# Second layer: ten pairs of projection blocks as seven half-products each, in another order

## The chip, the cores and the metric

The kernel runs on one core of one Trainium2 chip. The metric is the device time of one execution in microseconds (us). The median of three runs of the kernel before is 1501.39 us (1498.27 to 1502.47).

## The reference

Two layers are applied to 1024 latent tokens and 256 context tokens, each a row of 1024 values. A layer normalises and modulates the tokens, makes one input projection (1024 columns in, 3616 columns out: the pieces named below), feeds four groups of heads with it, and projects their gated outputs back. Cut to what matters here (calls shortened):

```python
def hybrid_layer(x, ctx, c, c_ctx, norm_g, w_mod, b_mod, w_in, ...):
    mod_x = jax.nn.silu(c) @ w_mod + b_mod
    ...
    hx = modulate(rms_norm(x, norm_g), sh_x, sc_x)
    hc = modulate(rms_norm(ctx, norm_g), sh_c, sc_c)
    (a_q, a_k, a_v, a_g, b_cq, b_ckv, b_kr, b_g,
     c_u, c_v, c_g, d_b, d_c, d_h, d_g) = jnp.split(hx @ w_in, IN_SPLIT_POINTS, axis=-1)
    (a_qc, a_kc, a_vc, ...) = jnp.split(hc @ w_in, IN_SPLIT_POINTS, axis=-1)
    out_a = neighbourhood_attention(heads(a_q), heads(a_k), heads(a_v), ctx keys and values, na_rpb)
    out_b = latent attention on b_cq, b_ckv and the rotated key b_kr
    out_c = spatial_gating(gelu(c_u), gelu(c_v), ...)   # u * (W_s LN(v) + b), in chunks of 128 tokens
    out_d = short_conv(d_b, d_c, d_h, sc_w)             # B * conv3(C * h)
    y = merge_branches([out_a, out_b, out_c, out_d], [a_g, b_g, c_g, d_g], w_out)   # gates through SiLU
    x = x + g_x * y
```

After the second layer only the latent tokens are wanted. Of the context tokens that layer needs the keys and values alone: the pieces ak, av, ckv and kr. The names in the kernel are those of the pieces without the underscore (a_k is ak); a piece of 256 columns is two blocks of 128, ak0 and ak1.

## The kernel before

**Tiling.** Everything is fp32. A product of two fp32 matrices is made of three: each operand is split into a high part (a cast to fp32r) and a low part (what the cast lost), and `mm3` (L172) issues high by high, high by low and low by high for each of 8 slices of the 1024 inputs. The normalised tokens lie in H, in tiles `g` that hold high and low of one slice (128 features) of one chunk. There are three chunks: 0 and 1 with 512 latent tokens each, 2 with the 256 context tokens. A weight block (128x1024) is loaded into `wr` by SP, `split` casts it on ScalarE (ACT) into `wh` (L338) and GpSimd (POOL) subtracts that into `wl` (L343). `proj` then takes 24 matmuls for each chunk into one bank of PSUM (`psb`, issued at L159) and hands the bank to a function that evacuates it. So a block on chunks 0 and 1 is 48 matmuls of 512 columns, and a pair of blocks is 96.

**Order in a layer.** The body of a layer emits cu and cv first: `cu` makes two blocks, `cv_tokens` makes 128 tokens at a time (24 matmuls of 256 columns), applies Gelu on ACT into a `v1` tile, and normalises it on VectorE (DVE): statistics (L479, L481), a reciprocal root whose power is on POOL (L204) and three steps on DVE (L206, L207, L209), then four subtract-and-multiply instructions (L486) into a `g` tile. The pool `v1` has three buffers, and the bias `bs` of the layer holds one. `cv_gate(c)` multiplies the four normalised token tiles of a chunk by a 128x128 matrix (16 small matmuls), adds the bias on DVE (L498) and multiplies into the map on POOL (L501). Then come cg; for j = 0, 1 dc, dh (with the convolution on POOL, L538, and DVE, L540 and L542), db, dg; av in ten tiles of 128 tokens, with copies of the values to scratch in DRAM; ckv with its own statistics (ones matmul on PE, L581 on DVE, power on POOL, transposes on PE); cq; the rotation of the key part of av's tiles on POOL (L650 to L655); ak; the transposes of the rotated keys; aq, bg, ag. `gate` is the evacuation of the gate blocks (Silu on ACT, L449, product on POOL, L451). Results that the attention reads go through tiles `st` (two buffers) to scratch in DRAM.

**What sets the order on an engine.** A scheduler orders each engine's instructions when the kernel is built, by times that it simulates. On the chip each engine takes its list strictly in that order and waits at the first instruction that isn't ready. The attention after the projections is in an order written out by hand, and neither it nor layer 1 is touched by the change.

The evacuation of a block and the split that feeds the next are these lines:

```python
hi, lo = w_block(a["wtb"][l, b_], scale, first_raw.get((l, b_)))
for c in chunks:
    p = PS("b", [CHUNKS[c][1]])
    mm3(p, [(hi[:, kc, :], lo[:, kc, :], hap(c, kc, 0), hap(c, kc, 1)) for kc in range(KC)])
    evac(c, p)
```

## Time and profile before

| | kernel before |
|---|---|
| median of 3 runs | 1501.39 us (1498.27 to 1502.47) |
| profiled execution, its own time | 1498.92 us |
| its span | 1496.8 us |
| mean granted clock of TensorE | 0.990 |
| busy: PE, DVE, ACT, POOL | 1427.9 us (95%), 767.5 (51%), 573.8 (38%), 459.7 (31%) |
| second layer's projections | about 822 to 1150 us of the span |

The span is from the first to the last instruction. A start in a timeline is counted from the span's start. Matmul rows give the time from issue to a modelled end, and these overlap: the rate of a stream of matmuls is the distance from start to start. "<-" behind a row names the work that released it after an idle stretch of its engine.

### The profile page before, as it was taken

The page shows a single profiled execution, that of the slowest core. Times are in us where ns is not written, and L with a number is a line of the kernel's source. Part 1 is how long each engine was busy: PE and PEld are TensorE (multiplying, and loading weights), DVE is VectorE, ACT ScalarE, POOL GpSimd, SP SyncE. Part 2 cuts the span into 40 slices and gives each one's busy share as a digit, 9 for nine tenths or more (in the row PEclk, how much of TensorE's full clock was granted, in tenths as well). Part 3 has the DMA queues.
Part 4 walks back from the last instruction along what each step waited for, and adds up shares of the span by engine and source line. Part 5 has one row for each costly group of instructions (what it writes and reads, how often), then busy time and mean ns, then how long its engine had stood idle before and what let it go on. Part 6 is the DMA issues. An engine that isn't in the chain of part 4 may idle for free.

```text
span 1496.8 us, 23098 instructions
## 1 busy us (share of the span) xinstructions
PE 1427.9 (95%) x8964; PEld 1193.6 (80%) x8964; DVE 767.5 (51%) x1873; ACT 573.8 (38%) x1303; POOL 459.7 (31%) x369
## 2 busy tenths in 40 slices
PE   4999999999998999999999999999999899999987
PEld 2888889988886777677788978898888677778887
DVE  5868656073026677564463752201213677754474
ACT  5512111122226565553442421112223666554542
POOL 2145343141230001536522253412232000155751
PEclk9999999999999999999999999999999999999999
DMA  9513325255361004746433101123474012385241
GB/s 350 199 41 113 120 81 173 99 210 167 127 126 15 1 22 126 152 123 166 140 115 127 36 29 43 54 84 122 155 242 90 1 36 43 99 179 160 71 155 56
DMA packets 80941, 166.45 MB, mean 111 GB/s; under 512 B 8128, under 2 KB 34752, under 8 KB 80704
## 3 DMA queue, kind: packets, MB, share of 16 engines
q1 hardware_dynamic: 63808, 136.66, 27.7%
q0 software_dynamic: 15936, 27.27, 9.1%
q8 instruction: 70, 1.15, 0.3%
q10 hardware_dynamic: 1088, 1.05, 0.2%
q14 instruction: 39, 0.32, 0.1%
HBM read 135.33 MB, written 33.82 MB: 113 GB/s over the span
## 4 chain that ended last, share of the span: by engine, by line
PE 82%; DVE 7%; ACT 3%; issue 3%; POOL 3%; DMA 1%; SPq 0%; DVEq 0%; POOLq 0%; ACTq 0%
PE psb L159 67%; PE pst L162 7%; PE psv L159 7%; PE pst L159 1%; DVE s L827 1%; ACT pt L723 1%; DVE g L486 1%; POOL g L1127 1%; POOL s L204 1%; DVE pt L721 1%; POOL wh L340 1%; DVE s L206 0%; DMA st<-in_nab 0%; DMA wr<-in_wtb 0%; POOL wl L343 0%
## 5 line engine op out<-in xcount | busy, mean ns | idle before, releaser
L159 PE MATMUL psb<-g,wh 128*128 128x512 f32 (+1 forms) x2400 | 685.2, 371 | 1.3 <-ACT g L394 1.3
L159 PEld LDWEIGHTS psb<-g,wh 128*128 128x128 f32 x2400 | 431.2, 189 | 85.7 <-ACT g L394 2.6
L159 PE MATMUL psb<-g,wl 128*128 128x512 f32 (+1 forms) x1200 | 443.5, 370 | 0.0
L159 PEld LDWEIGHTS psb<-g,wl 128*128 128x128 f32 x1200 | 226.1, 188 | 41.3 <-issue 1.0
L343 POOL TENSOR_TENSOR wl<-wr,wh 128x1024 fp32r<-128x1024 f32 (+2 forms) x64 | 149.9, 2344 | 305.2 <-ACT wh L338 297.9
L159 PE MATMUL psb<-g,st 128*128 128x512 f32 (+1 forms) x616 | 159.7, 377 | 17.2 <-DVE g L763 4.5
L827 DVE TENSOR_REDUCE s<-psb 128x1 f32<-128x512 f32 (+1 forms) x200 | 117.2, 591 | 83.7 <-PE psb L159 80.7
L159 PE MATMUL psb<-g,g 128*128 128x256 f32 (+2 forms) x832 | 136.0, 309 | 0.1
L159 PEld LDWEIGHTS psb<-g,st 128*128 128x128 f32 x616 | 96.9, 190 | 43.8 <-issue 14.2
L723 ACT COPY pt<-pst 128x512 f32<-128x512 f32 (+1 forms) x132 | 73.8, 559 | 126.5 <-PE pst L162 126.2
L159 PE MATMUL psv<-pt,g 128*64 128x256 f32 (+1 forms) x1312 | 120.8, 334 | 0.8 <-DVE s L972 0.5
L338 ACT CAST wh<-wr 128x1024 fp32r<-128x1024 f32 (+2 forms) x56 | 56.1, 1006 | 167.4 <-PE psb L159 134.7
L159 PEld LDWEIGHTS psb<-g,g 128*128 128x128 f32 x832 | 113.5, 197 | 6.0 <-issue 3.3
L159 PEld LDWEIGHTS psv<-pt,g 128*64 128x64 f32 x1312 | 79.9, 137 | 32.7 <-issue 9.0
L318 DVE CUSTOM_DVE_ANT_0 tmp<-g,x 128x512 f32<-128x512 f32 x112 | 94.7, 898 | 8.7 <-POOL x L451 7.2
L721 DVE COPY pt<-pst 128x512 f32<-128x512 f32 x132 | 86.2, 653 | 10.0 <-PE pst L162 9.4
L162 PE MATMUL pst<-ident,g 128*128 128x128 f32 x464 | 82.2, 278 | 8.1 <-ACT g L974 3.2
L204 POOL TENSOR_TENSOR s<-s,mhalf 128x4 f32<-128x4 f32 (+3 forms) x35 | 35.7, 1020 | 150.2 <-DVE s L260 59.3
L340 POOL TENSOR_SCALAR wh<-wr 128x1024 fp32r<-128x1024 f32 x16 | 44.3, 2770 | 114.6 <-PE pst L162 66.3
L1157 DVE SCALAR_TENSOR_TENSOR x<-psb,modG,x 128x512 f32<-128x512 f32 (+1 forms) x48 | 29.5, 616 | 91.9 <-PE psb L159 58.2
L162 PEld LDWEIGHTS pst<-ident,g 128*128 128x128 f32 x464 | 55.5, 140 | 25.4 <-ACT g L974 5.3
L159 PE MATMUL psb<-st,g 128*128 128x288 f32 (+1 forms) x456 | 64.3, 289 | 0.0
(183 smaller groups left out, 1837.4 us busy)
## 6 DMA issues: line engine op xcount, KB each, us to landing
g<-in_wmod SPq DMA_DIRECT2D x48, 512.0 KB, 4.5
wr<-in_wtb SPq DMA_DIRECT2D x46, 512.0 KB, 3.8
wr<-in_wout SPq DMA_DIRECT2D x27, 512.0 KB, 3.7
st<-in_nab SPq DMA_DIRECT2D x24, 384.0 KB, 3.5
x<-in_xT SPq DMA_DIRECT2D x32, 256.0 KB, 5.9
g<-scr_q POOLq DMA_DIRECT2D x32, 256.0 KB, 7.0
x<-x SPq DMA_DIRECT2D x24, 256.0 KB, 2.8
g<-scr_k POOLq DMA_DIRECT2D x20, 256.0 KB, 5.4
```

The source lines that it names most:

```text
L159: return self._next(nc.tensor.matmul(*p, **k))
L162: return self._next(nc.tensor.transpose(*p, **k))
L204: pool.tensor_tensor(r0, v, mhalf[:, :n], ALU.pow)
L318: dve.tensor_tensor_reduce(junk, w[:, hf * 512:hf * 512 + 512], crow[cond, hf], 1.0, 0.0, ALU.mult, ALU.add, part[:, i, cond, hf:hf + 1])
L338: act.copy(hi, raw)
L340: pool.tensor_scalar(hi, raw, 1.0, None, ALU.mult)
L343: (pool if lo_eng == "pool" else dve).tensor_tensor(lo, raw, f(hi), ALU.subtract)
L486: dve.tensor_scalar(vns[c][:, i, g, :], gv[:, g, :], mv[:, g, 0:1], r[:, g:g + 1], ALU.subtract, ALU.mult)
L721: dve.tensor_copy(dst, src)
L723: act.copy(dst, src)
L827: dve.reduce_max(st["mx"][:, i:i + 1], s_, AX.X)
L1157: dve.scalar_tensor_tensor(xa, p, mod[l]["G"][:, fb, cond:cond + 1], xa, ALU.mult, ALU.add)
```

## The change

Only layer 2 is changed. Layer 1 keeps the blocks and their order; its code moves into a function `standard`.

**Half-products.** For ten pairs of blocks (cg, dc, dh, db, dg, cq, ak, aq, bg, ag) the two weight blocks and the two latent chunks are read as a 2 by 2 matrix of halves: rows of weights j = 0, 1, halves k = 0, 1 of the 1024 inputs (4 slices each), chunks 0 and 1. Where before the pair was eight half-products of 12 matmuls, `proj2` makes seven of 12, with sums of halves as operands (Strassen's scheme in Winograd's form). Four sums of weight halves are made on DVE for each pair (L693 to L696), and seven half blocks are split by `w_op` (a cast of 128x512 on ACT, a subtraction of 128x512 on POOL) where before two whole blocks were. Between the products ACT and DVE move and add partial results (L701, L703, L708, L713, L718, L721), and an evacuation then often reads SBUF where it read PSUM.

**Token sums.** `right_sums(i)`, for i = 0 to 3, makes the sums of the tokens' halves that all ten pairs use: per i four additions of high and low (L669, three on DVE, one on POOL), four subtractions on DVE (L672) and four splits (cast on ACT, low part on DVE for two and on POOL for two).

**Context.** ak on chunk 2 is made on its own by `block_c`, with its own load of the blocks. **Buffers.** A class `Phase` opens pools for a part of the program: four tiles `o` for some of the sums during the projections, `pt` and `pc` at the beginning and in the attention. The rotated keys and the convolution's input move from `g` to `x` tiles. **Order.** After cu and cv come ckv (chunks 2, 1, 0), ak on the context, av (context tiles, then chunk 1, then chunk 0), the rotation, and the pairs cg, dc, dh, db, dg, cq, ak, aq, bg, ag; `mla_load` and the first attention unit's loads are emitted inside ag.

The diff, cut to its core:

```diff
+    BUFS = {"x": 20, "g": 24, "wr": 2, "wh": 2, "wl": 2, "st": 2, "tmp": 6, "pt": 6, "v1": 3, "pc": 8, "s": 12, "o": 4}
...
+        def w_op(raw):
+            t = T(("wh", "wl")[nop[0] % 2], [2, 512], F32R)
+            nop[0] += 1
+            split(t[:, 0, :], t[:, 1, :], raw)
+            return t.rearrange("p h (k n) -> p h k n", k=4)
+
+        R = {}
+
+        def right_sums(i):
+
+            t = {}
+            for k, (c, kc) in enumerate(((0, i), (1, i), (1, i + 4), (0, i + 4))):
+                t[k] = T("x", [512])
+                (pool if k == 3 else dve).tensor_tensor(t[k], f(H[c, kc][:, 0, :]), f(H[c, kc][:, 1, :]), ALU.add)
+            R["11", i], R["21", i], R["22", i] = H[0, i], H[0, i + 4], H[1, i + 4]
+            for name, o, p_, q_ in (("1", 0, 1, 0), ("3", 1, 2, 1), ("2", 2, 2, 0), ("4", 3, 3, 2)):
+                dve.tensor_tensor(t[o], t[p_], t[q_], ALU.subtract)
+                r = R[name, i] = T("o" if i < 2 and name in "23" else "g", [2, 512], F32R)
+                split(r[:, 0, :], r[:, 1, :], t[o], lo_eng="dve" if name in "12" else "pool")
+
+        def product(p, w, name, first=True):
+            n = 0
+            for i in range(4):
+                r = R[name, i]
+                for wl_, rl_ in ((0, 0), (0, 1), (1, 0)):
+                    pe.matmul(p, w[:, wl_, i, :], r[:, rl_, :], start=first and n == 0, stop=n == 11,
+                              skip_group_check=True)
+                    n += 1
+
+        def proj2(base, evac, mid=None):
+            r = {}
+            for j in range(2):
+                for k in range(2):
+                    r[j, k] = T("x", [512])
+                    sp.dma_start(r[j, k], a["wtb"][l, BLOCKS.index(f"{base}{j}")][:, k * 512:(k + 1) * 512])
+            q = T("wr", [2, 512])
+            a11, a12 = w_op(r[0, 0]), w_op(r[0, 1])
+            dve.tensor_tensor(q[:, 1, :], r[0, 0], r[1, 0], ALU.subtract)
+            dve.tensor_tensor(r[1, 0], r[1, 0], r[1, 1], ALU.add)
+            dve.tensor_tensor(q[:, 0, :], r[1, 0], r[0, 0], ALU.subtract)
+            dve.tensor_tensor(r[0, 1], r[0, 1], q[:, 0, :], ALU.subtract)
+            s2, s1 = w_op(q[:, 0, :]), w_op(r[1, 0])
+            x_, y_ = PS("b", [512]), PS("b", [512])
+            product(x_, a11, "11")
+            m1 = T("tmp", [512])
+            act.copy(m1, x_)
+            product(y_, a12, "21")
+            dve.tensor_tensor(m1, y_, m1, ALU.add)
+            evac(0, m1, 0)
+            s3 = w_op(q[:, 1, :])
+            product(x_, s2, "2", False)
+            u2 = T("tmp", [512])
+            act.copy(u2, x_)
+            s4 = w_op(r[0, 1])
+            z_ = PS("b", [512])
+            product(z_, s1, "1")
+            z5 = T("tmp", [512])
+            dve.tensor_copy(z5, z_)
+            if mid is not None:
+                mid()
+            a22 = w_op(r[1, 1])
+            product(x_, s3, "3", False)
+            dve.tensor_tensor(z5, x_, z5, ALU.add)
+            evac(1, z5, 1)
+            product(z_, s4, "22", False)
+            dve.tensor_tensor(u2, z_, u2, ALU.add)
+            evac(1, u2, 0)
+            product(x_, a22, "4", False)
+            evac(0, x_, 1)
...
+        def paired():
+            right_sums(0)
+            right_sums(1)
+            cv_gate(1)
+            proj("ckv0", (2, 1, 0), ckv_evac)
+            for j in range(2):
+                block_c(f"ak{j}", 2, lambda c, p: k_evac(c, p, j))
+            wav = w_tok(a["wav"][l], 288)
+            for t in (8, 9, 4, 5, 6, 7):
+                av_tile(t, wav)
+            right_sums(2)
+            right_sums(3)
+            for t in range(4):
+                av_tile(t, wav)
+            av_windows()
+            kr = kr_rotate()
+            proj2("cg", lambda c, p, j: gate(c, p, 4 + j))
+            kr_transpose(*kr)
+            proj2("dc", lambda c, p, j: act.copy(map_(6 + j, c), p))
...
+            proj2("dh", conv_in)
...
+            proj2("db", mulb)
+            proj2("dg", lambda c, p, j: gate(c, p, 6 + j))
+            proj2("cq", cq_evac)
+            proj2("ak", k_evac)
+            cq_stats()
+            proj2("aq", lambda c, p, j: q_evac(c, p, j, 0.125))
+            proj2("bg", lambda c, p, j: act.activation(map_(2 + j, c), p, AF.Silu))
...
+            ph = Phase("prj", ("o",))
+            paired()
+        else:
+            standard()
+            ag_weights()
...
-            mla_load()
-        for c in order[:-1]:
-            ag(c)
-            if c == 2:
-                mla_load()
-        units[0].prep()
-        ag(order[-1])
+            proj2("ag", lambda c, p, j: act.activation(map_(j, c), p, AF.Silu), lambda: (mla_load(), units[0].prep()))
+            ph.close()
```

**Where instructions move, on DVE.** In cv's token tiles of chunk 0, before (s are statistics, v is a Gelu tile, g the normalised tokens; s_8499 belongs to the second tile, v_8533 to the third):

```order
L483 TENSOR_SCALAR s_8495<-s_8486 128x4
L206 SCALAR_TENSOR_TENSOR s_8499<-s_8495,s_8497 128x4
L207 TENSOR_TENSOR s_8499<-s_8499,s_8497 128x4
L209 SCALAR_TENSOR_TENSOR s_8502<-s_8499,s_8497 128x4
L479 BN_STATS s_8535<-v_8533 128x6 x3
L486 TENSOR_SCALAR g_8407<-v_8483,s_8486,s_8502 128x64 x4
L479 BN_STATS s_8535<-v_8533 128x6
L481 BN_AGGR s_8536<-s_8535 128x2 x4
L483 TENSOR_SCALAR s_8545<-s_8536 128x4
L206 SCALAR_TENSOR_TENSOR s_8549<-s_8545,s_8547 128x4
```

After (x, o and g are token sums; s_8562 belongs to the third tile v_8546, and v_8596 is the fourth):

```order
L672 TENSOR_TENSOR x_8913<-x_8913,x_8911 128x512
L672 TENSOR_TENSOR x_8937<-x_8937,x_8935 128x512
L357 TENSOR_TENSOR o_8924<-x_8911,o_8924 128x512
L220 SCALAR_TENSOR_TENSOR s_8562<-s_8558,s_8560 128x4
L672 TENSOR_TENSOR x_9410<-x_9410,x_9408 128x512
L357 TENSOR_TENSOR o_8948<-x_8935,o_8948 128x512
L672 TENSOR_TENSOR x_9434<-x_9434,x_9432 128x512
L221 TENSOR_TENSOR s_8562<-s_8562,s_8560 128x4
L223 SCALAR_TENSOR_TENSOR s_8565<-s_8562,s_8560 128x4
L493 BN_STATS s_8598<-v_8596 128x6 x3
L500 TENSOR_SCALAR g_8420<-v_8546,s_8549,s_8565 128x64 x4
L493 BN_STATS s_8598<-v_8596 128x6
```

What moved: these rows are the end of a stretch that begins behind the second tile's first step (L220 after, L206 before); from there to the statistics of v_8596 all 12 additions L669, all 16 subtractions L672 and two low parts (L357) stand between the steps of the second and the third tile.

**On PE, at the gate of cv.** Before, the gate of chunk 0 is followed by cg:

```order
L159 MATMUL psb_8813<-g_8069,g_8272 128x256
L159 MATMUL psb_8863<-tmp_8330,g_8407 64x128 x8
L159 MATMUL psb_8875<-tmp_8330,g_8407 64x128 x8
L159 MATMUL psb_8893<-g_7677,wh_8889 128x512 x2
L159 MATMUL psb_8893<-g_7677,wl_8890 128x512
L159 MATMUL psb_8893<-g_7682,wh_8889 128x512 x2
```

After, the matmuls of chunk 0's gate (g_8420) and the first of chunk 1's (g_8675) stand together, and ckv on the context (psb_8985) follows:

```order
L173 MATMUL psb_8826<-g_8082,g_8285 128x256
L173 MATMUL psb_8876<-tmp_8343,g_8420 64x128 x6
L173 MATMUL psb_8888<-tmp_8343,g_8420 64x128 x6
L173 MATMUL psb_8876<-tmp_8343,g_8420 64x128 x2
L173 MATMUL psb_8888<-tmp_8343,g_8420 64x128 x2
L173 MATMUL psb_8955<-tmp_8343,g_8675 64x128 x2
L173 MATMUL psb_8967<-tmp_8343,g_8675 64x128
L173 MATMUL psb_8985<-g_8307,wh_8981 128x256 x2
L173 MATMUL psb_8985<-g_8307,wl_8982 128x256
```

What moved: three small matmuls on the fifth token tile, the first of chunk 1, now stand ahead of the first block; before, they came after cg0 on both chunks (48 matmuls).

**On PE and POOL, at the rotated keys.** Before, the transposes of the rotated keys (tile g_10142) stand on PE between two blocks, the rotation that makes them much earlier on POOL:

```order
L159 MATMUL psb_10335<-g_8321,wh_10273 128x256 x2
L159 MATMUL psb_10335<-g_8321,wl_10274 128x256
L162 MATMUL pst_10364<-ident_66,g_10142 128x128 x4
L162 MATMUL pst_10373<-ident_66,g_10142 128x128 x4
L159 MATMUL psb_10395<-g_7677,wh_10391 128x512 x2
L159 MATMUL psb_10395<-g_7677,wl_10392 128x512
```

```order
L604 TENSOR_TENSOR x_10035<-x_10035,tmp_10103 128x512
L650 TENSOR_TENSOR tmp_10144<-tmp_9545,tmp_9546 128x256
L652 TENSOR_TENSOR tmp_10144<-tmp_9545,tmp_9546 128x16x8 x2
L655 COPY tmp_10143<-tmp_9545 128x2x32 x4
L343 TENSOR_TENSOR wl_10274<-wr_10271,wh_10273 128x1024
L604 TENSOR_TENSOR x_10066<-x_10066,tmp_10135 128x512
L654 TENSOR_TENSOR g_10142<-tmp_10144 128x8x32 x4
```

After, the transposes (x_9572, x_9573, tmp_9574) follow the last tile of av (psb_9539) directly and stand ahead of the first half-product of cg (psb_9616):

```order
L173 MATMUL psb_9539<-wl_9221,g_7725 128x288
L173 MATMUL psb_9539<-wh_9220,g_7725 128x288
L176 MATMUL pst_9733<-ident_66,x_9572 128x128 x4
L176 MATMUL pst_9742<-ident_66,x_9573 128x128 x4
L176 MATMUL pst_9751<-ident_66,tmp_9574 128x128 x2
L173 MATMUL psb_9616<-g_7690,wh_9600 128x512 x2
L173 MATMUL psb_9617<-g_7710,wl_9603 128x512 x2
```

On POOL the rotation, which reads the key part of all ten tiles of av, is followed by the first split of cg's weights (wh_9600):

```order
L357 TENSOR_TENSOR g_9449<-x_9434,g_9449 128x512
L631 TENSOR_TENSOR tmp_9575<-tmp_8900,tmp_8901 128x256
L633 TENSOR_TENSOR tmp_9575<-tmp_8900,tmp_8901 128x16x8 x2
L638 COPY tmp_9574<-tmp_8900 128x2x32 x4
L636 TENSOR_TENSOR x_9572<-tmp_9575 128x4x32
L636 TENSOR_TENSOR x_9573<-tmp_9575 128x4x32
L636 TENSOR_TENSOR x_9572<-tmp_9575 128x4x32
L636 TENSOR_TENSOR x_9573<-tmp_9575 128x4x32
L636 TENSOR_TENSOR x_9572<-tmp_9575 128x4x32
L636 TENSOR_TENSOR x_9573<-tmp_9575 128x4x32
L636 TENSOR_TENSOR x_9572<-tmp_9575 128x4x32
L636 TENSOR_TENSOR x_9573<-tmp_9575 128x4x32
L357 TENSOR_TENSOR wh_9600<-x_9591,wh_9600 128x512
L357 TENSOR_TENSOR wl_9603<-x_9593,wl_9603 128x512
```

What moved: the rotation and the transposes had blocks of cq and ak around them, and now lie between av and the first pair.

## Rows read from the trace of the kernel before

**Rows 1.** The page: busy time, share of the span and instructions of each engine.
```profile
PE 1427.9 (95%) x8964; PEld 1193.6 (80%) x8964; DVE 767.5 (51%) x1873; ACT 573.8 (38%) x1303; POOL 459.7 (31%) x369
```
**Rows 2.** Busy time in windows: window, sum, then PE, PEld, DVE, ACT, POOL, clock.
```profile
850.00:875.00 25.00, 25.00 (x179) 22.52 (x178) 18.99 (x90) 6.29 (x10) 11.65 (x10) 1.00 0.13 43
...
925.00:950.00 25.00, 25.00 (x110) 20.25 (x109) 0.00 (x0) 4.26 (x6) 9.75 (x5) 1.00 0.13 43
```
**Rows 3.** Timeline of PE inside a stream of blocks: start, duration, instruction.
```profile
1049.20 0.64 PE L159 MATMUL psb<-g,wh 128*128 128x512 f32 x2
...
1058.96 0.64 PE L159 MATMUL psb<-g,wh 128*128 128x512 f32 x2
```
**Rows 4.** Timeline of PE at the gate of chunk 0.
```profile
862.38 2.08 PE L159 MATMUL psb<-tmp,g 128*64 128x128 f32 x32
864.39 0.74 PE L159 MATMUL psb<-g,wh 128*128 128x512 f32 x2
```
**Rows 5.** Timeline of DVE, token preparation; the first row is from the tokens' normalisation.
```profile
827.68 3.40 DVE L393 SCALAR_TENSOR_TENSOR tmp<-x,modA,tmp 128x512 f32<-128x512 f32 x5 [0.17 <-ACT tmp L263]
...
852.32 2.35 DVE L206 SCALAR_TENSOR_TENSOR s<-s,s 128x4 f32<-128x4 f32 x1 [1.18 <-POOL s L204]
...
865.35 1.25 DVE L206 SCALAR_TENSOR_TENSOR s<-s,s 128x4 f32<-128x4 f32 x1 [0.53 <-POOL s L204]
...
867.97 1.60 DVE L486 TENSOR_SCALAR g<-v,s,s 128x64 f32<-128x64 f32 x4
```
**Rows 6.** Timeline of POOL in the same stretch.
```profile
852.26 2.39 POOL L343 TENSOR_TENSOR wl<-wr,wh 128x1024 fp32r<-128x1024 f32 x1
...
864.31 1.01 POOL L204 TENSOR_TENSOR s<-s,mhalf 128x4 f32<-128x4 f32 x1 [2.63 <-DVE s L483]
865.29 1.30 POOL L501 TENSOR_TENSOR x<-x,tmp 128x512 f32<-128x512 f32 x1
```
**Rows 7.** Groups by line and shape, POOL, 850 to 1150 us: busy us, mean ns.
```profile
L538 POOL TENSOR_SCALAR x<-g,vecs 128x512 f32<-128x512 f32 x4 | 7.4, 1844 | 12.8 <-DVE g L531 12.8
...
L343 POOL TENSOR_TENSOR st<-wr,st 128x576 fp32r<-128x576 f32 x2 | 3.3, 1658 | 0.0
...
L343 POOL TENSOR_TENSOR g<-st,g 128x512 fp32r<-128x512 f32 x1 | 1.3, 1289 | 4.4 <-ACT g L338 4.4
```
**Rows 8.** Timeline of DVE: one round of ckv's statistics.
```profile
1023.34 0.16 DVE L581 TENSOR_SCALAR s<-pst 128x4 f32<-128x4 f32 x1 [10.83 <-PE pst L159]
1024.65 0.16 DVE L206 SCALAR_TENSOR_TENSOR s<-s,s 128x4 f32<-128x4 f32 x1 [1.15 <-POOL s L204]
...
1025.04 0.16 DVE L209 SCALAR_TENSOR_TENSOR s<-s,s 128x4 f32<-128x4 f32 x1
```
**Rows 9.** DMA issues, 850 to 1150 us: count, KB each, median us to landing.
```profile
wr<-in_wtb SPq DMA_DIRECT2D x18, 512.0 KB, 3.7
scr_vw<-scr_v SPq DMA_DIRECT2D x4, 512.0 KB, 5.8
...
g<-scr_ck POOLq DMA_DIRECT2D x2, 512.0 KB, 8.5
...
scr_k<-st SPq DMA_DIRECT2D x2, 256.0 KB, 4.3
```
**Rows 10.** Timeline of POOL: the rotation of the keys.
```profile
1048.44 0.74 POOL L650 TENSOR_TENSOR tmp<-tmp,tmp 128x256 f32<-128x256 f32 x1
1049.14 0.88 POOL L652 TENSOR_TENSOR tmp<-tmp,tmp 128x128 f32<-128x128 f32 x2
1049.96 0.76 POOL L655 COPY tmp<-tmp 128x64 f32<-128x64 f32 x4
```
**Rows 11.** Windows of 2 us around an idle stretch of PE; PEclk is the third from the end.
```profile
1162.00:1164.00 2.00, 0.00 (x0) 0.00 (x0) 1.17 (x3) 0.79 (x3) 0.00 (x0) 1.00 0.00 0
1164.00:1166.00 2.00, 1.74 (x10) 1.53 (x11) 0.74 (x3) 1.75 (x6) 0.00 (x0) 0.88 0.00 0
1166.00:1168.00 2.00, 2.00 (x12) 2.00 (x11) 0.00 (x0) 2.00 (x7) 0.00 (x0) 0.50 0.00 0
```

More of the change, by code (lines that the diff above doesn't have):

```diff
@@ L106, in backbone, with __init__, close @@
     uid = [0]
[L108 removed]
+    home = {}
+    class Phase:
+        def __init__(self, name, tags):
+            self.cm, self.tags = tc.tile_pool(name=name, bufs=1, reuse_waits="tile"), tags
+            p = self.cm.__enter__()
+            home.update({t: p for t in tags})
+        def close(self):
+            for t in self.tags:
+                del home[t]
+            self.cm.__exit__(None, None, None)
+    BUFS = {"x": 20, "g": 24, "wr": 2, "wh": 2, "wl": 2, "st": 2, "tmp": 6, "pt": 6, "v1": 3, "pc": 8, "s": 12, "o": 4}
     SIZE = {"x": 512, "g": 1024, "wr": 1024, "wh": 1152, "wl": 1152, "st": 1152, "tmp": 512, "pt": 512,
[L110 removed]
+            "v1": 256, "pc": 256, "s": 40, "o": 1024}
     def T(tag, shape, dt=F32):
@@ L558, in layer, with av_tile @@
         sp.dma_start(tabt, a["tabt"])
-        for t in range(10):
+        def av_tile(t, wav):
             p = PS("b", [288])
@@ L565, in layer, with av_windows @@
             dve.tensor_copy(KR[:, t, :], p[:, 256:288])
-        for cb in range(4):
-            spill(scr["vw"][cb].rearrange("(r c) n -> r c n", c=32),
-                  scr["v"][:SEQ, :].rearrange("(r c) n -> r c n", c=64)[:, KCS[cb]:KCS[cb] + 32, :])
+        def av_windows():
+            for cb in range(4):
+                spill(scr["vw"][cb].rearrange("(r c) n -> r c n", c=32),
+                      scr["v"][:SEQ, :].rearrange("(r c) n -> r c n", c=64)[:, KCS[cb]:KCS[cb] + 32, :])
         def ckv_evac(c, p):
@@ L594, in cq_evac @@
             o, n = CHUNKS[c]
-            sq = T("tmp" if j else "x", [512])[:, :n]
-            if j == 0:
-                cqsq[c] = sq
+            second = c in cqsq
+            sq = T("tmp" if second else "x", [512])[:, :n]
+            cqsq.setdefault(c, sq)
             act.activation(sq, p, AF.Square)
@@ L602, in cq_evac @@
             spill(scr["cq"][:, j * 128:(j + 1) * 128, o:o + n].rearrange("h p n -> p h n"), f(st))
-            if j:
+            if second:
                 pool.tensor_tensor(cqsq[c], cqsq[c], sq, ALU.add)
         cqsq = {}
-        for j in range(2):
-            proj(f"cq{j}", all_chunks, lambda c, p: cq_evac(c, p, j))
         def cq_stats():
@@ new lines, in kr_transpose @@
+        def kr_transpose(KRd, KRc):
+            for c in range(3):
+                o, n = CHUNKS[c]
+                nt = n // 128
+                pk = PS("t", [nt, 128])
+                for i in range(nt):
+                    pe.transpose(pk[:, i, :], KRd[c][:, i, :] if c < 2 else KRc[:, i, :], ident)
+                st = T("st", [2, 512], F32R)[:, :, :n]
+                act.copy(st[64:128, 0, :], pk[64:128])
+                dve.tensor_tensor(st[64:128, 1, :], pk[64:128], f(st[64:128, 0, :]), ALU.subtract)
+                spill(scr["kr"][:, :, o:o + n].rearrange("h p n -> p h n"), f(st[64:128]))
@@ new lines, in product @@
+        def product(p, w, name, first=True):
+            n = 0
+            for i in range(4):
+                r = R[name, i]
[43 more added lines that the diff above has]
+            evac(0, x_, 1)
@@ L679, in ag, with ag_weights @@
+        agw = []
+        def ag_weights():
+            agw.extend(w_block(a["wtb"][l, BLOCKS.index(f"ag{j}")]) for j in range(2))
         def ag(c):
@@ L1211, in layer @@
         if last:
-            mla_load()
-        for c in order[:-1]:
-            ag(c)
-            if c == 2:
-                mla_load()
-        units[0].prep()
-        ag(order[-1])
+            proj2("ag", lambda c, p, j: act.activation(map_(j, c), p, AF.Silu), lambda: (mla_load(), units[0].prep()))
+            ph.close()
+        else:
+            for c in order[:-1]:
+                ag(c)
+                if c == 2:
+                    mla_load()
+            units[0].prep()
+            ag(order[-1])
+        ph = Phase("att", ("pt", "pc"))
         queue, ends = [], []
@@ L1289, in backbone @@
     raws = {}
+    ph = Phase("begin", ("pt",))
     for op in STARTUP:
```

157 lines of the change are left out of this document (91 added, 66 removed).

## The prediction

> **What bounds the kernel now.** I read the busy line of the page first, then the busy time in windows over layer 2's projections, then single timelines. PE is busy 95% of the span, the next engine 51% [rows 1]. In the projections PE is busy in every microsecond of a window, at clock 1.00, with POOL at 40% and DVE between nothing and three quarters [rows 2]. So here a matmul taken away is time won, as long as nothing makes PE wait; and whatever makes PE wait is time lost at once, since PE has no idle time of its own in which to hide it. The reader should see in [rows 2] both halves of the question: there is room on POOL and DVE on average, and yet in the first window, where the tokens are prepared, DVE already works 19.0 of 25 us. The change puts its largest new load on DVE into just that window.
>
> All sums are made against the profiled execution, 1498.92 us, which is 2.5 us below the median of 1501.39. I add the 2.5 at the end.
>
> **The gain.** Ten pairs go from 96 to 84 matmuls of 512 columns: 120 fewer. From 1049.20 to 1058.96 lie 42 matmuls [rows 3], so one takes 9.76/42 = 0.232 us, and 120 take **27.9 us**. The context part of ckv and ak is as large as before and moves only.
>
> **The start: the token sums on DVE.** Before, the gate of chunk 0 runs on PE at 862.4 and cg follows at 864.4 [rows 4]; the fifth token tile is normalised at 868 to 869.6 [rows 5], while PE works on cg. After, by the order listed for PE, the gate of chunk 0 needs the third and fourth token tiles, and three matmuls on the fifth stand ahead of ckv. By the order listed for DVE, 30 instructions of 128x512 (12 additions, 16 subtractions, 2 low parts) stand between the second tile's first step and the third's normalisation. They start at 852.3, where DVE is free of the second tile's wait [rows 5]. Each reads two SBUF operands; five such instructions took 3.40 us [rows 5], 0.68 each, so 30 take 20.4. Before, DVE came from 852.3 to the end of the fifth tile in 17.3 us [rows 5], some 4 of which were waits for POOL's power that the sums now fill. So without any disturbance the fifth tile is done at about 852.3 + 17.3 + 20.4 - 4 = 886, and PE, which wanted ckv at 864.4, loses **21 us**.
>
> POOL disturbs. The tiny step L206 (128x4) took 2.35 us while POOL's split of 2.39 us ran, and 1.25 us while a POOL product of 1.30 us ran; its sister took 0.16 [rows 5, 6]. So a DVE instruction with two SBUF operands stood still for the whole of a POOL instruction that had begun just before it. In this stretch POOL's new work ahead of the fifth tile is four additions and two low parts of 128x512, six times 1.29 [rows 7] = 7.7 us, and the old split and products, which before met a DVE with little to do, now meet a full queue: 2.4 + 2 x 1.3 = 5.0, of which 3.3 was paid before (2.35 + 1.25 less two times 0.16). If all of it is serial, 9.4 us are added: **30 us**. I take **29**, near the upper end, because both rows show the full block; I keep 19 to 31 (0.60 instead of 0.68 an instruction gives 2 less).
>
> [...]
>
> **From ckv to av.** ckv (14 us of PE) and ak on the context (6 us) now come ahead of av, and three things end late. ak1's split on POOL, 2.4 us like that of [rows 6], is queued behind the gate's products: about 2.7 us of PE. The statistics of ckv's last two chunks are rounds of PE, DVE, POOL's power, DVE and PE: from the first to the last DVE step 1.9 us [rows 8]; before, blocks stood between them on PE, now two rounds stand one behind the other, 4 us or more. And av's first weights go through the two `st` tiles, which ak's context results have just filled: a spill of 256 KB lands after 4.3 us [rows 9], and then come two low parts of 128x576, 1.66 each [rows 7], on POOL: about 8.4 us behind ak, with the statistics inside them. With 2 us for the second half of the weights that is **13 us**, between 6 (only the statistics and one split count) and 20 (nothing overlaps).
>
> **The rotated keys.** Before, the rotation ran on POOL beside blocks on PE. After, it can begin when av's last tile is copied, and the transposes stand on PE ahead of cg's first product. POOL: 0.74 + 0.88 + 0.76 [rows 10], then eight additions of 128x128 at half of 0.88, 3.5: 5.9 us. With the copy ahead, the transposes, their evacuation and the split wh_9600 (1.29, [rows 7]) behind them: 8 to 9 us. Beside it, cg's weights wait in SP's queue behind four copies of scratch (`vw`) that wait for av's last spill: 5.8 for a copy, 3.7 for a load [rows 9], then a cast and a split, some 11 to 14 if nothing overlaps. I take **10**, and keep 7 to 14.
>
> **The steady pairs.** PE takes 84 x 0.232 = 19.5 us for a pair. POOL: seven low parts, 9.0, and for a gate pair four products of 1.30, together 14.2. DVE with two SBUF operands: four sums, 2.7, and some evacuations that now read SBUF. Added up as if they excluded each other, 17 to 18 us: under PE's 19.5, so hidden. Only dh is above: 9.0 + 4 x 1.84 [rows 7] on POOL and 12 convolution steps, 8 of them long, on DVE (5.4) and the sums (2.7) make 24.5. So **4 us**, between 0 and 8. PSUM: a bank is evacuated during the next product of 12 x 0.232 = 2.8 us, against about 0.7 for one evacuation: nothing.
>
> **The end.** The loads of ck, cq and kr need `g` tiles that the token sums hold until ag has read them. Before, these loads were out early; a load lands after 8.5 us [rows 9], with ag's remaining products beside it: **3 us**, 0 to 8.
>
> **The clock.** [...]
>
> **Sum.** -27.9 + 29 + 13 + 10 + 4 + 3 + 7 = +38. 1498.9 + 38 + 2.5 = **1539 us**. All lower ends: -27.9 + 19 + 6 + 7 + 0 + 0 + 4 = +8, 1509; all upper ends: -27.9 + 31 + 20 + 14 + 8 + 8 + 12 = +65, 1566.
>
> **Rivals.**
> (1) *The two engines share instead of excluding each other.* Then the start costs 21, the splits in the middle come sooner (10) and the steady pairs cost nothing: -27.9 + 21 + 10 + 9 + 0 + 2 + 6 = +20, 1521. Against it stand the two blocked rows. Chance 0.15.
> (2) *The products win: faster.* The one mechanism is the start: were the third to fifth token tiles ready before the sums ran, PE would go straight into ckv and the 20 to 30 us would vanish, the sums running beside ckv's 14 and ak's 6 us of matmuls. Then -27.9 + 0 + 6 + 7 + 0 + 0 + 2 = -13, 1488. It decides from the point where all waits together fall under 23 us. For it speaks only that DVE has room later [rows 2]; against it the order of DVE's list, in which the sums are first. Chance 0.13.
> (3) *The steady pairs are bound by DVE and POOL together.* If evacuations from PSUM are blocked too, about 12 more DVE instructions a pair at 0.7 come into the serial sum: 17.5 + 8.4 = 26 us, 6 over PE. With half of the pairs affected, 25 to 30 us more than the 4 above, less what no longer waits elsewhere: about 1560. Chance 0.10.
> (4) *The gain is not there*, because a product on 4 slices runs slower than one on 8: the stream would have to lose its rate at each switch of banks, and the rows show no gap between blocks (25.00 of 25 us busy across several switches, [rows 2]). Under 0.02, and on the slow side.
> [...]
>
> **How the numbers follow.** My forecast, 1539 with 1522 to 1560 around it, has 0.55; rival 1 0.15, rival 3 0.10, rival 2 0.13; the rest, 0.07, is a time within 0.3% or little above, where the start costs 19 and nearly nothing else counts. Differences within 0.3% (4.5 us) can't be told from no change here. So faster 0.13, same 0.05, slower 0.82. The range leaves out rival 2 and the tail of rival 3: 1499 to 1566.
>
> **What would show it.** In the profile of the changed kernel: PE idle from about 862 to about 890, released by DVE (g, L500); a second stretch of waits ahead of av, released by POOL (st, L357) or a spill; a third ahead of cg, released by POOL (x, L636), or by a load; then products at 2.8 us each without waits except in dh and dg; the granted clock down after each of the stretches. DVE's L669 and L672 at more than 0.7 us where POOL runs would confirm the block. I am wrong if PE is busy at 870, if the waits ahead of av and cg are under 10 us together, or if cg to ag take much more than 10 x 19.5 us.

## The result and the profile after

The changed kernel takes 1559.42 us (median of 4 runs, 1554.21 to 1560.25) against 1500.59 us (1498.27 to 1502.47): the ratio is 1.0386, 95% interval 1.0358 to 1.0413, so it is 58.8 us slower. Forecast were 1539 us, a range of 1499 to 1566, and slower with 0.82. The time lies in the range, 20 us above the forecast; these 20 us are the question of the experiments.

The page after, busy time and the granted clock in 40 slices (compare [rows 1]):

```profile
PE 1422.3 (91%) x8844; PEld 1182.8 (76%) x8844; DVE 869.5 (56%) x1991; ACT 616.3 (40%) x1393; POOL 540.5 (35%) x443
...
PEclk9999999999999999999999688899999999999999
```

120 matmuls are gone, and PE's busy time fell by 5.6 us only (1427.9 to 1422.3), not by 27.9. The larger part of the missing 22.3 us went to matmuls at the lower clock: PE's busy time multiplied by what the granted clock lacks of 1.00 is 25.7 us over the whole span after and 11.2 before, 14.5 more. The clock line shows where, in the slices from 860 to 1010 us.

Windows of the stretch, as in [rows 2] (window, sum, PE, PEld, DVE, ACT, POOL, clock, DMA):

```profile
850.00:875.00 25.00, 12.75 (x105) 12.10 (x104) 23.81 (x42) 4.01 (x7) 12.94 (x8) 0.83 0.10 34
875.00:900.00 25.00, 11.49 (x62) 9.36 (x63) 19.00 (x81) 3.27 (x8) 9.22 (x9) 0.55 0.00 1
900.00:925.00 25.00, 21.46 (x129) 17.61 (x127) 6.23 (x29) 4.93 (x9) 8.99 (x7) 0.93 0.04 12
925.00:950.00 25.00, 13.79 (x72) 13.01 (x73) 5.99 (x14) 5.81 (x11) 8.45 (x6) 0.60 0.29 97
...
975.00:1000.00 25.00, 14.47 (x51) 10.82 (x52) 11.84 (x11) 7.14 (x12) 14.50 (x21) 0.73 0.57 195
...
1050.00:1075.00 25.00, 20.96 (x80) 16.52 (x79) 22.54 (x27) 4.59 (x8) 18.62 (x11) 0.86 0.13 43
```

In the first window DVE is busy 23.8 of 25 us and PE half of it. The waits themselves, from the timeline of PE (start, duration, instruction, idle before and what ended it):

```profile
870.55 1.12 PE L173 MATMUL psb<-tmp,g 128*64 128x128 f32 x8 [8.92 <-ACT v L489]
881.06 0.91 PE L173 MATMUL psb<-tmp,g 128*64 128x128 f32 x4 [9.39 <-DVE g L500]
...
892.32 1.10 PE L173 MATMUL psb<-tmp,g 128*64 128x128 f32 x6 [6.27 <-DVE g L500]
918.09 0.58 PE L173 MATMUL psb<-g,wl 128*128 128x256 f32 x1 [1.93 <-POOL wl L357]
925.63 1.09 PE L176 MATMUL pst<-ident,s 128*128 128x128 f32 x4 [2.24 <-DVE s L223]
930.62 1.09 PE L176 MATMUL pst<-ident,s 128*128 128x128 f32 x4 [2.40 <-DVE s L223]
938.15 1.57 PE L173 MATMUL psb<-st,g 128*128 128x288 f32 x5 [6.45 <-ACT st L352]
941.46 5.77 PE L173 MATMUL psb<-st,g 128*128 128x288 f32 x29 [1.73 <-POOL st L357]
...
980.62 1.97 PE L176 MATMUL pst<-ident,x 128*128 128x128 f32 x8 [5.94 <-POOL x L636]
983.17 0.69 PE L176 MATMUL pst<-ident,tmp 128*128 128x128 f32 x2 [0.59 <-DVE st L650]
988.00 1.22 PE L173 MATMUL psb<-g,wh 128*128 128x512 f32 x2 [4.13 <-ACT wh L352]
...
1059.16 3.36 PE L173 MATMUL psb<-g,wl 128*128 128x512 f32 x7 [4.04 <-POOL wl L357]
...
1207.76 1.40 PE L173 MATMUL psb<-g,st 128*128 128x512 f32 x3 [3.52 <-DMA g<-scr_kr]
```

The reader should see the forecast's places one after the other: the gate of cv (three long waits), the statistics and `st` ahead of av, the rotation and the weights ahead of cg, the wait behind dh's convolution (1059), and the loads at the end. The first long wait is put down to ACT's Gelu, which itself stood behind DVE:

```profile
870.12 0.38 ACT L489 ACTIVATE v<-psb 128x256 f32<-128x256 f32 x1 [0.34 <-DVE s L495]
```

PE reached the gate at 861.6 (862.4 before, [rows 4]) and ckv at 893.35, where the kernel before went on at 864.39.

The queue that holds the gate, from DVE's timeline, and POOL's beside it:

```profile
852.68 2.38 DVE L669 TENSOR_TENSOR x<-g 128x512 f32<-128x512 f32 x2
854.98 1.24 DVE L221 TENSOR_TENSOR s<-s,s 128x4 f32<-128x4 f32 x1
856.14 9.39 DVE L669 TENSOR_TENSOR x<-g 128x512 f32<-128x512 f32 x10
...
866.65 2.47 DVE L672 TENSOR_TENSOR x<-x,x 128x512 f32<-128x512 f32 x4
...
870.23 3.27 DVE L672 TENSOR_TENSOR x<-x,x 128x512 f32<-128x512 f32 x4
```

```profile
851.44 6.54 POOL L669 TENSOR_TENSOR x<-g 128x512 f32<-128x512 f32 x4
857.94 2.83 POOL L357 TENSOR_TENSOR wl<-wr,wh 128x1024 fp32r<-128x1024 f32 x1
```

Four subtractions of DVE take 2.47 us alone and 3.27 where a POOL low part falls among them; ten additions take 9.39 instead of about 6 (0.61 each with POOL idle, in the run with the sums on DVE only, below), and POOL's four 6.54 instead of 5.2 (1.29 each, [rows 7]). Both engines take longer than alone. DVE ran its list in the order listed ahead: L357 at 877.58, L220 at 878.18, L672 at 878.25, L357 at 878.85, L672 at 879.45, L221 at 880.06, L223 at 880.24.

### The profile page after: what moved, and what is told of

Its sections match the earlier page's. It is cut to its first block, busy times and chain, and to the rows that moved or that the text cites. A ratio compares the mean times of both kernels' runs of the same rounds, so it can differ in the third digit from the quotient of the medians.

```text
span 1556.9 us, 23285 instructions
## 1 busy us (share of the span) xinstructions
PE 1422.3 (91%) x8844; PEld 1182.8 (76%) x8844; DVE 869.5 (56%) x1991; ACT 616.3 (40%) x1393; POOL 540.5 (35%) x443
## 5 line engine op out<-in xcount | busy, mean ns | idle before, releaser
L173 PE MATMUL psb<-g,wh 128*128 128x512 f32 (+1 forms) x2120 | 579.6, 370 | 6.2 <-ACT wh L352 5.3
L173 PEld LDWEIGHTS psb<-g,wh 128*128 128x128 f32 x2120 | 382.7, 191 | 80.9 <-ACT wh L352 6.4
L173 PE MATMUL psb<-g,wl 128*128 128x512 f32 (+1 forms) x1240 | 414.2, 376 | 10.0 <-POOL wl L357 7.3
L173 PEld LDWEIGHTS psb<-g,wl 128*128 128x128 f32 x1240 | 236.7, 192 | 57.5 <-POOL wl L357 8.9
L357 POOL TENSOR_TENSOR wl<-wr,wh 128x1024 fp32r<-128x1024 f32 (+2 forms) x48 | 111.9, 2334 | 191.2 <-ACT wh L352 190.2
L352 ACT CAST wh<-wr 128x1024 fp32r<-128x1024 f32 (+2 forms) x50 | 45.6, 917 | 111.8 <-PE psb L173 77.8
```

The costliest lines, as they stand in the source:

```text
L173: return self._next(nc.tensor.matmul(*p, **k))
L352: act.copy(hi, raw)
L357: (pool if lo_eng == "pool" else dve).tensor_tensor(lo, raw, f(hi), ALU.subtract)
```

## The experiments

Each of the seven runs up to "Put together" is a single execution, to be read against 1559.4 us and the scatter of the changed kernel's own four runs (1554.21 to 1560.25 us); positions of different runs are compared as distances or as waits, since the start of layer 2 moves by some us from run to run.

**Without the sums.**

```diff
-            for name, o, p_, q_ in (("1", 0, 1, 0), ("3", 1, 2, 1), ("2", 2, 2, 0), ("4", 3, 3, 2)):
-                dve.tensor_tensor(t[o], t[p_], t[q_], ALU.subtract)
...
+            for name, (c, kc) in (("11", (0, i)), ("21", (0, i + 4)), ("22", (1, i + 4)), ("1", (1, i)),
+                                  ("2", (1, i + 4)), ("3", (0, i + 4)), ("4", (1, i))):
+                R[name, i] = H[c, kc]
```

> The changed kernel without the token sums: the products read the token tiles of H in place of the sums, so no L669, L672 or their splits run (this leaves out a part of the computation). Theory: the stretch from PE's arrival at the gate (861.6) to the first matmul of ckv (893.4) shrinks from 31.7 us to 5 to 9, because only DVE's queue held PE there; ckv to av keeps 8 us or more of waits, cg keeps about 10; total 1517 to 1532. Rival (the new place of the gate's matmuls on PE costs the time, not the sums): the stretch stays above 20 us and the total above 1545.

Measured: 1528.43 us. Waits on PE's timeline:

```profile
869.87 1.11 PE L173 MATMUL psb<-tmp,g 128*64 128x128 f32 x6 [4.50 <-DVE g L500]
...
912.57 1.57 PE L173 MATMUL psb<-st,g 128*128 128x288 f32 x5 [6.47 <-ACT st L352]
...
963.37 1.22 PE L173 MATMUL psb<-g,wh 128*128 128x512 f32 x2 [5.17 <-ACT wh L352]
```

From PE's arrival at the gate to ckv's first matmul lie 7.6 us (863.30 to 870.91). At the gate 25.8 us of waits (8.92 + 9.39 + 0.26 + 0.92 + 6.27) became 4.5, and the total fell by 31. The waits ahead of av and cg stayed. So the first term comes from the token sums; that it is their place on DVE, and not their work, is shown by the run with the sums behind the tokens, below.

**The order alone, with whole blocks.**

```diff
-            a11, a12 = w_op(r[0, 0]), w_op(r[0, 1])
...
+                    hi, lo = ws[j]
...
+                    p = PS("b", [512])
+                    mm3(p, [(hi[:, kc, :], lo[:, kc, :], hap(c, kc, 0), hap(c, kc, 1)) for kc in range(KC)])
+                    evac(c, p, j)
```

> The new order of blocks alone: no token sums, and each pair as eight half-products in whole blocks of 24 matmuls as before the change. Theory: PE gets its 27.9 us back as work, the pairs run without waits (the 10 us of waits in the pairs of the changed kernel go), and the exposed stretches of the order stay (ckv to av 8 us or more, ahead of cg about 10, restarts of the clock): 1525 to 1540, that is slower than the kernel before by the price of the order alone, and 5 to 15 us above the run without sums. Rival (the order is free and all of the loss comes with the products and sums): 1500 to 1506.

Measured: 1527.17 us. Waits on PE's timeline:

```profile
872.76 1.10 PE L173 MATMUL psb<-tmp,g 128*64 128x128 f32 x6 [4.50 <-DVE g L500]
...
915.41 1.57 PE L173 MATMUL psb<-st,g 128*128 128x288 f32 x5 [6.46 <-ACT st L352]
918.71 5.72 PE L173 MATMUL psb<-st,g 128*128 128x288 f32 x29 [1.73 <-POOL st L357]
```

The new order costs 27 us by itself, 17.9 of them waits: 4.5 at the gate, 0.9 at ak1's split, then the same 2.2, 2.1, 6.5 and 1.7 us ahead of av as in the run without sums. The expectation that this run lies 5 to 15 us above the run without sums was wrong, it lies 1.3 below. Between av and cg it has no wait at all, and none in the pairs: with whole blocks the weights are loaded early and the transposes of the keys come later (from 974 us). So the products without their sums save 27.9 us of PE and lose as much to waits that are their own: ahead of cg, in the pairs, and in the clock behind them. The expectation had put the waits ahead of cg down to the order; they came with `proj2`, its loads and the place that the scheduler then gave to the transposes.

**The sums behind the tokens.**

```diff
+                    tok[0] = dve.tensor_scalar(vns[c][:, i, g, :], gv[:, g, :], mv[:, g, 0:1], r[:, g:g + 1],
+                                               ALU.subtract, ALU.mult)
...
+                if k < 3:
+                    after(m, tok[0])
```

> The changed kernel with one dependency more: DVE's additions of the token sums stand behind the normalisation of the last token tile. Same work. Theory: the stretch at the gate shrinks from 31.7 us to 5 to 9, but DVE then runs the sums while ckv's statistics wait for it, so part comes back ahead of av: total 1530 to 1547, av's matmuls in full stream at 920 to 932 instead of 941.5. Rival (the sums cost nothing but their place, and everything behind shifts by the whole 25 us): 1528 to 1534, av at 916. Rival (the sums are not what PE waits for): 1555 to 1562.

Measured: 1546.43 us; av in full stream at 930.5, both within the theory.

```profile
867.76 1.10 PE L173 MATMUL psb<-tmp,g 128*64 128x128 f32 x6 [4.49 <-DVE g L501]
...
910.26 0.69 PE L176 MATMUL pst<-ident,s 128*128 128x128 f32 x2 [13.93 <-DVE s L223]
```

The wait at the gate went, and 13.9 us came back one stage later, where ckv's statistics now stand behind the sums on DVE. A long block on an engine that runs its list in order must be placed against everyone who waits on that engine, not against one: 8.9 + 9.4 + 6.3 us at the gate before, 13.9 us at ckv's statistics here.

**The sums on DVE only.**

```diff
-                (pool if k == 3 else dve).tensor_tensor(t[k], f(H[c, kc][:, 0, :]), f(H[c, kc][:, 1, :]), ALU.add)
+                dve.tensor_tensor(t[k], f(H[c, kc][:, 0, :]), f(H[c, kc][:, 1, :]), ALU.add)
...
-                split(r[:, 0, :], r[:, 1, :], t[o], lo_eng="dve" if name in "12" else "pool")
+                split(r[:, 0, :], r[:, 1, :], t[o], lo_eng="dve")
```

> The changed kernel with all additions and low parts of the token sums on DVE, none on POOL: at the gate DVE has six instructions of 128x512 more in its queue, POOL six fewer. Theory (a DVE instruction with two SBUF operands and a POOL instruction exclude each other): POOL's six took 1.3 to 1.6 us of DVE's time each, DVE needs 0.60 for each, so the first matmul of ckv comes 3 to 7 us earlier than 893.4. Rival (the engines share, DVE is merely long): it comes 3 to 5 us later. The total follows by about as much, 1550 to 1557 against 1562 to 1566.

Measured: 1557.72 us, ckv's first matmul at 894.0. PE reached the gate at 865.0 here and at 861.6 in the changed kernel, so as a distance the stretch is 29.0 us instead of 31.7: 2.7 shorter, just short of the theory's 3 to 7, where the rival had it longer. Against PE's arrival the sums also began 1.1 us later, because POOL's split of 2.4 us now stood ahead of them. The total is 1.7 us less, within the scatter, and decides nothing. The durations do decide:

```profile
858.44 7.91 DVE L669 TENSOR_TENSOR x<-g 128x512 f32<-128x512 f32 x13
```

Thirteen additions in 7.91 us are 0.61 each, with POOL idle (16.43 us up to 873.66, the row below), against 0.94 above. So the two engines did hold each other up. In the changed kernel POOL's four additions and the three of DVE that fall among them end after 6.54 us; POOL's alone would be 5.2, and all seven one after the other 4 x 1.29 + 3 x 0.60 = 7.0. How much of the total this costs was not settled by this run.

POOL's and DVE's timelines of this run show one more thing in the statistics of the gate, the reciprocal root of a 128x4 tile on POOL:

```profile
873.66 4.39 POOL L218 TENSOR_TENSOR s<-s,mhalf 128x4 f32<-128x4 f32 x1 [16.43 <-DVE s L497]
```

```profile
875.29 1.89 DVE L672 TENSOR_TENSOR x<-x,x 128x512 f32<-128x512 f32 x3
878.08 0.16 DVE L220 SCALAR_TENSOR_TENSOR s<-s,s 128x4 f32<-128x4 f32 x1 [0.90 <-POOL s L218]
```

The other eight such instructions between 850 and 950 us take 1.04 on average; this one takes 4.39, as long as DVE's subtractions follow each other without a gap, and ends 0.87 us after the last of them. DVE's next step of the chain stands behind it. So with the additions off POOL the gate's chain grew by some 3.3 us at another place, which may be one reason that the total hardly fell.

**ckv's results in a tile of their own.**

```diff
-    BUFS = {"x": 20, "g": 24, "wr": 2, "wh": 2, "wl": 2, "st": 2, "tmp": 6, "pt": 6, "v1": 3, "pc": 8, "s": 12, "o": 4}
+    BUFS = {"x": 20, "g": 24, "wr": 2, "wh": 2, "wl": 2, "st": 2, "tmp": 6, "pt": 6, "v1": 3, "pc": 8, "s": 12, "o": 5}
-            st = T("st", [2, 512], F32R)[:, :, :n]
+            st = T("o" if last else "st", [2, 512], F32R)[:, :, :n]
```

> The changed kernel, but the results of ckv and of ak on the context go to scratch from a fifth tile of the pool o in place of the two st tiles that av's first weights need. Theory: the two waits ahead of av (6.45 us for the cast and 1.73 us for the low part into st) and the two waits for ckv's statistics (2.2 and 2.4 us) go or get covered by av's matmuls; av's matmuls are in full stream 8 to 13 us earlier against ckv's start (48 us there, 35 to 40 here), total 1545 to 1552. Rival (the POOL queue, not the tiles, holds av's weights): the distance stays above 45 us and the total at 1556 to 1562.

Measured: 1539.37 us, 20 us less, more than expected. From ckv's first matmul (897.1) to av's first (919.5) lie 22.4 us, where 44.8 lay before (893.35 to 938.15):

```profile
919.46 3.35 PE L173 MATMUL psb<-st,g 128*128 128x288 f32 x24
```

No wait is left from ckv to av. The two `st` tiles had held back av's weights, and the transposes of ckv's statistics, which stood bare because of it, now lie among av's matmuls. The clock stays at 1.00 from 902 to 950, where it was 0.60 in [925, 950] above. The 20 us add up: 14.8 us of waits are gone, the time lost to the lower clock from ckv's start to 950 fell from 8.1 to 1.0 us, and the waits at the gate were 2.5 us longer (28.3).

**Transposes behind cg, cg's weights early.**

```diff
+                        after(m, lastp[0])
...
+            cgw = [w_load(a["wtb"][l, BLOCKS.index(f"cg{j}")]) for j in range(2)]
```

> The changed kernel, but the transposes of the rotated keys stand on PE behind cg's products, and cg's two weight blocks are loaded into the wr tiles ahead of av's second half, not behind the copies of scratch. Theory: from av's last matmul (974.4) to cg's first (988.0) PE lost 13.6 us to these two; now 0 to 3, and one restart of the clock less: total 1543 to 1549. Rival (the rotation on POOL still stands ahead of cg's splits and takes the place of the wait): 5 to 8 us stay, 1550 to 1555.

Measured: 1547.58 us, within the theory's range; no wait between av and cg is left on PE's timeline. A part came back within cg, where the wait for a low part on POOL grew from 1.34 to 2.89 us.

**PE kept busy at the gate.**

```diff
+                fill(30)
...
+                    fill(36 if ii[0] == 0 else 24)
```

> The changed kernel with 90 matmuls of 512 columns more, into a spare bank that nobody reads: 30, 36 and 24 of them stand in PE's three long waits at the gate (8.9, 9.4 and 6.3 us before), so that PE is busy there. Theory (the waits are DVE's, and the idle PE costs more through its clock): ckv starts at the same time within 2 us, the matmuls behind it run at the full clock at once, and the total falls by 2 to 6 us although PE has 20.9 us of work more: 1553 to 1557. Rival (the clock behind the waits is no cost of its own): 1559 to 1565.

Measured: 1554.41 us. This run is inconclusive on the clock. Only the first fill lay in a wait; the other two came behind the second:

```profile
886.48 1.12 PE L173 MATMUL psb<-tmp,g 128*64 128x128 f32 x8 [11.02 <-ACT v L489]
887.53 10.31 PE L173 MATMUL pst<-g 128*128 128x512 f32 x36
```

ckv began 40.2 us after PE's arrival instead of 31.7, so the theory's condition was not met, although the total lies in its range. What can be said is that PE's own delay of 8.5 us at this place cost nothing: from ckv's first matmul to av in full stream lie 35.8 us instead of 48.1. Of these 12.4 us less, 5.7 are waits that were gone (9.0 instead of 14.75) and 5.5 are time lost to the lower clock (0.8 instead of 6.25); the clock behind the fills was whole:

```profile
894.00:898.00 4.00, 4.00 (x21) 3.06 (x22) 2.78 (x18) 0.39 (x1) 1.01 (x1) 1.00 0.02 6
...
902.00:930.00 28.00, 27.21 (x179) 23.06 (x178) 11.98 (x38) 5.71 (x10) 10.94 (x9) 1.00 0.07 20
```

**Put together.** v9 takes the edits of the three runs above that helped (sums behind the tokens, ckv's results in their own tile, transposes behind cg), puts the gate of chunk 1 behind ckv's first block, and the convolution's first factor on ACT. v10 moves all sums to DVE; v11 moves the rotation of the keys from cg's splits behind dc's; v12 emits a pair's first splits ahead of the last product of the pair before.

```diff
-                    pool.tensor_scalar(m, z[j, c], w[1], None, ALU.mult)
+                    act.activation(m, z[j, c], AF.Copy, scale=w[1])
...
-            proj2("dc", lambda c, p, j: act.copy(map_(6 + j, c), p))
-            kr_transpose(*kr)
+            proj2("dc", lambda c, p, j: act.copy(map_(6 + j, c), p))
+            kr = kr_rotate(lasts[0])
```

> The same products and sums as in the changed kernel, with what the other runs change put together: sums on DVE behind the tokens and behind ckv's statistics, chunk 1's gate behind the first ckv block, ckv's results in their own tile, cg's weights ahead, rotation and transposes behind cg, and the convolution's first factor on ACT in place of POOL. Theory (the waits of the changed kernel are all of this kind): nothing but the pairs' 6 us, the end's 4 us and little of the clock stays, so most of the 27.9 us comes through: 1482 to 1498, faster than the kernel before. Rival (DVE and POOL together have too much work in 860 to 930, and whatever is moved waits elsewhere): 1503 to 1525.

> The run v9 with all token sums on DVE: POOL loses four additions and eight low parts of 128x512, DVE gets them; on DVE the first quarter of the sums stands behind the tokens, the rest behind ckv's statistics. Theory (the two engines exclude each other, so that a piece costs their common time 1.29 us on POOL and 0.60 on DVE, 8 us less in all, and POOL's splits for cg no longer stand behind the sums): the 5.9 us wait of cg's product for POOL's low part and the 4.0 us wait for the statistics' transposes shrink to 0 to 3 us together, with one restart of the clock less: 1494 to 1503. Rival (DVE alone becomes the bound and the sums come too late for cg): PE waits 5 us or more for DVE in cg, total 1506 to 1513.

> The run v10 with the rotation of the keys on POOL behind the splits of dc instead of those of cg, and the transposes behind dh. In v10 POOL ran the rotation from 949.3 to 956.5 ahead of dc's first low part, and PE waited 5.9 us for that. Theory (POOL has 16 of 19.5 us to do in dc with the rotation, against 21 in cg): the wait goes, with one restart of the clock, 6 to 9 us less than v10: 1497 to 1501, the same as the kernel before. Rival (the rotation delays dh's splits by as much): 1503 to 1508.

> The run v11 with the next pair's first two weight splits emitted ahead of the last product of a pair. In v10 the casts of a next pair stood on ACT behind the evacuation of the last product, and PE waited 1.2 to 2.1 us at three such places (4.5 us). Theory: these waits go, 3 to 5 us less than v11. Rival (the casts wait for the weights' loads or for a buffer, wherever they stand in the list): within 1.5 us of v11.

| run | median us | ratio to before, 95% interval |
|---|---|---|
| v9 | 1509.36 | 1.0063 (1.0040 to 1.0086) |
| v10 | 1505.99 | 1.0048 (1.0032 to 1.0064) |
| v11 | 1492.49 | 0.9944 (0.9922 to 0.9966) |
| v12 | 1493.70 | 0.9955 (0.9942 to 0.9969) |

v9 missed its range and lies in its rival's (1503 to 1525): a wait of 5.9 us for a low part on POOL stood behind cg, and I took POOL's share of the sums for its cause. v10 missed its range too and shows that it was not: with all sums on DVE the same 5.9 us were there. POOL's timeline of v10 names the cause, the rotation that I had moved ahead of dc's first split:

```profile
953.20 3.32 POOL L647 TENSOR_TENSOR x<-tmp 128x128 f32<-128x128 f32 x8
956.49 1.25 POOL L362 TENSOR_TENSOR wl<-x,wl 128x512 fp32r<-128x512 f32 x1
```

v11 moved it once more and is 13.5 us faster, more than the 6 to 9 expected. The wait is gone, and with it 3.0 us that PE had lost to the lower clock behind it; PE's waits from 845 to 1225 us add up to 19.9 us instead of 29.8, so other waits shrank as well. v11 is faster than the kernel before by 0.56% (0.34 to 0.78), a small gain but clear of the scatter. v12's edit changed nothing that can be measured, as its rival said. v11 still has these waits on PE in the same stretch (engine, line, total, count, longest):

```profile
PE pst L176 <- DVE tmp L551: 2.7, 1, 2.7
...
PE psb L173 <- DMA g<-scr_kr: 2.2, 2, 1.7
```

So of the 27.9 us 8.4 come through in the best version that was run.

## Why the prediction was right, and where its sizes were off

- **The gain.** 120 matmuls fewer (8964 to 8844), as counted. No run prices them alone; the order with whole blocks and the run without sums differ by nothing, for the reason given there. But the trace shows the rate: between the two rows below lie 168 matmuls of the pairs without a wait, 39.07/168 = 0.2326 us each, as in [rows 3]. So the 27.9 us are there, and the fourth rival is refuted.

```profile
1080.34 1.54 PE L173 MATMUL psb<-o,wh 128*128 128x512 f32 x6
...
1119.41 0.63 PE L173 MATMUL psb<-g,wh 128*128 128x512 f32 x2
```

- **The start, 29 us.** Measured 28.96 (893.35 against 864.39). The order of DVE's list, read instruction by instruction, gave the place, the engine that ends the wait and nearly the size: 25.8 us are waits, and 3.0 are the gate's own matmuls at the lower clock, which the prediction had in another term. So the agreement to a tenth is luck; the queue itself cost about 26, between the 21 without the block and the 30 with all of it. The runs without the sums and with the sums later show the cause.
- **From ckv to av, 13 us.** The waits are 14.8 (1.93 + 2.24 + 2.40 + 6.45 + 1.73), at the three places that were worked out. But the stage lost some 8 us more through the clock, and the fix was worth 20.
- **The keys, 10 us.** Waits of 5.94 + 0.59 + 4.13 = 10.7. Right in size, and the rotation, the transposes and the loads were the places named; that the order of blocks alone does not bring them was learnt from the run with whole blocks.
- **The pairs, 4 us.** The wait behind dh's convolution on POOL was 4.04 us, as predicted; it falls in db's first product. The others were missed: two casts of a next pair that stand on ACT behind an evacuation (1.19 us each), a low part that came late in cg (1.34), and two banks of PSUM that ACT or DVE had not yet emptied (0.68 and 1.10), a term that the prediction had put at nothing. In all 10.1 us of idle PE from 988 to 1195, outside the 0 to 8.
- **The end, 3 us.** 3.5 us for the load of kr and 0.4 for ck.
- **The clock, 7 us: the step that failed.** The 7 us were my estimate, four or five restarts at the 1.2 us or more of the one isolated wait in [rows 11] (0.12 x 2 + 0.50 x 2). No run shows that term; the runs showed 16.2 us in its place. In the changed kernel the granted clock was 0.50 in every window of 4 us from 870 to 894, at the gate, and again from 926 to 942, ahead of av, and the matmuls between the waits and just behind them ran at 0.50 of the full clock. Windows of 4 us after (the clock is the third from the end):

```profile
870.00:874.00 4.00, 1.12 (x8) 0.72 (x8) 4.00 (x11) 0.85 (x2) 1.49 (x2) 0.50 0.00 0
...
886.00:890.00 4.00, 0.05 (x1) 0.00 (x0) 1.80 (x5) 1.35 (x3) 3.53 (x4) 0.50 0.00 0
...
894.00:898.00 4.00, 4.00 (x20) 3.60 (x20) 2.78 (x18) 0.38 (x1) 1.01 (x1) 0.57 0.00 0
...
926.00:930.00 4.00, 2.21 (x12) 2.13 (x10) 1.53 (x4) 0.62 (x1) 1.32 (x1) 0.50 0.01 5
```

PE's busy time multiplied by what the clock lacks of 1.00, added up in slices of about 1 us from 861.6 to 1215.7, is 19.2 us, 3.0 of them inside the start's 29. It falls into six stretches of 5.0, 1.6, 4.5, 3.7, 2.7 and 1.7 us. So this term was 16, not 7, and outside its 4 to 12, and the pairs were 10.1, not 4: 9 and 6 of the 20 us that were missing. With the other stages the account nearly closes: 29.0 + 14.8 + 10.7 + 10.1 + 3.9 + 16.2 - 27.9 = 56.8, against 58.8 measured. That the closeness of the waits is what kept the clock low is my reading of these rows and was not shown: the run with PE kept busy, which was to show it by itself, mixes it with fewer waits. The nearest to a price is ckv's own tile, where 7.1 of 20 us are the clock's.

The rival of sharing engines is refuted by the durations (0.94 against 0.61) and by the start, which cost more than its 21; the rival of winning products is refuted by the gate, and v11 shows its condition: once the waits are away, the products win. The third rival, pairs bound by DVE and POOL together, named 1560 us, and 1559.4 was measured; that is coincidence. It needed 25 to 30 us more in the pairs than the 4, and evacuations from PSUM that POOL blocks. The pairs lost 6 us more, and the evacuations were not slowed (0.692 us on average at L718, as for dh's at L531 in the kernel before, 0.692), while weight sums with two SBUF operands were (1.325 us on average at L696, where an addition took 0.68 with POOL idle; 985 to 1205 us, groups by line and shape):

```profile
L696 DVE TENSOR_TENSOR x<-x,wr 128x512 f32<-128x512 f32 x10 | 13.2, 1325 | 11.7 <-POOL wh L357 6.4 <-POOL wl L357 5.1
...
L718 DVE TENSOR_TENSOR tmp<-psb,tmp 128x512 f32<-128x512 f32 x10 | 6.9, 692 | 25.1 <-PE psb L173 25.0
```

## What to carry to other kernels

A saving on the busiest engine is worth what it leaves after the waits that its preparation makes, and these can be read from the instruction order before anything runs: find the long block, list what stands behind it on its in-order engine, and ask who waits for each of those. Where several waits follow closely on TensorE, price them together with its clock, not one by one (16.2 us here, where the count of single restarts gave 7). When a block is moved out of one wait, look at the next consumer of the same engine before counting the gain: two of the moves here (the sums behind the tokens, the rotation behind cg) carried the wait to the next stage.
